# Where modulation's sums, the latents' products and head 0's evictions stand in a two-layer retention and attention kernel

## The chip, the cores and the metric

The kernel runs on one core of a Trainium2 chip, in one launch. The metric is the time of one execution on the device in microseconds (us). All arithmetic that the reference does is done on the chip in 32-bit numbers; a matmul of such numbers is made of three products of a high and a low part (high by high, high by low, low by high), so every operand is first split into `hi` and `lo`.

Five engines matter. PE does the matmuls and writes sums into PSUM banks. DVE and ACT do the elementwise work, read PSUM and make the high and low parts: ACT copies the high part, DVE subtracts it from the whole to get the low part. SP issues loads, POOL issues stores and some tiny powers. Each engine takes its instructions in the order of its own list, so an instruction that waits holds back all that stand behind it on that engine.

## The reference, cut to what matters

```python
c_act = silu(c)
for i in range(2):                       # layer 0: retention, layer 1: latent attention
    mod = c_act @ ada_w[i] + ada_b[i]    # modulation: 3 x 2048 numbers a layer
    shift, scale, gate = split(mod, 3)
    h = rmsnorm(x, norm_g[i]) * (1 + scale) + shift
    y = retention_branch(h) if i == 0 else mla_branch(h)
    x = x + gate * y
return rmsnorm(x, final_norm_g)
```

There are 512 tokens of width 2048. Retention has 8 heads: for each, queries and keys (2 x 256 columns) are turned by a rotary table; scores of keys and queries, times a decay, multiply the values (512 columns); the result is normalised over each head's columns and multiplied by a SiLU gate (512 columns), and all heads go through one output projection. Latent attention projects h to two latents of 512 columns, a rotary key and a gate of 2048 columns, expands the latents to 16 heads and does causal softmax attention.

`mod` is a matrix-vector product: each of its 128-row groups needs a load of 128 x 2048 weights, a product with `silu(c)` and a sum along the row. The kernel does it on DVE.

## The kernel before, in words

**Stages, in order of time.** First the tokens' norm, layer 0's first modulation, and head 0's `qk`, values and gates in one interleaved sweep over the width (to about 160 us). Then a list called `steps`, which is walked in order: head 5's `qk` as a plain step list (`qk_steps(5)`); for each head 1 to 4 fourteen narrow steps (`narrow_qk`) for its queries and keys, then sixteen steps for its values and gates (`heads_steps`); for heads 5, 6, 7 the sixteen alone; then plain steps for `qk` of heads 6 and 7; then four rounds of sixteen steps, n = 0 to 3, of the output projection (`round_steps`), beside which retention itself runs; then layer 1: gate columns in plain steps (`g2_steps`), the latents as sixteen steps again, two more groups of gates, attention, and the last projection.

**Sixteen steps: `seven_steps`** (L766 on). A product of 1024 by 1024 blocks is done with seven multiplications instead of eight. The first eight steps (u = 0 to 7, the first sweep) add to four pairs of banks: x and s, in the four banks tagged `acc`; z and y, in the four tagged `aux`. Two of each are used by every head, so a head's first product into a bank waits until the head before has emptied it. The second sweep, again u = 0 to 7, adds to x, y and s only; z has been copied out at its start. After u = 7 of the second sweep `finish` empties x and s by ACT (L641) and adds y to two saved tiles by DVE (L988, L990). In a first-sweep step the groups of three matmuls per bank are listed x, s, z, y (two banks each); for u = 0 the list is reordered to z, x, y, s, for the heads and for the latents (`"c"`, which come from the same function). The step's weights arrive as two tiles, e and o; `prepare` combines them on DVE and splits them (L802 to L809 first sweep, L814 to L819 second).

**Narrow steps** (`narrow_steps`, L852 on) do a head's queries and keys the same way with half-width products: per group of pairs one step for `b11`, then three steps (`o`, `a`, `b`) twice; two such groups make fourteen steps of 24 matmuls of 256 columns. The preparation of `a` needs four DVE combinations (L931 to L935) before its split (L874, L875).

**The walk over `steps`** (end of the function) writes, for step i and in this order: SP's weight loads for up to three units ahead and the loads set beside the step; the preparation (split) of the weights of steps up to i + `lead` (1, or 2 around the narrow steps) on DVE and ACT; the work set beside it under `form`; the step's matmuls, then matmuls set beside it (scores, values, transposes); then the DVE sums of modulation whose operands were fetched in the step before; then one load for each of the next step's `rows`; then the step's `follow` (evictions). Each block on an engine is queued behind the last instruction written for that engine. So `step.rows` is how many sums of modulation are done after that step, and their loads are written at the end of the step before.

**Modulation's sums.** `all_rows` yields 8 x 2 tiles for each of eight pieces: three pieces (48 sums) while heads 1 to 7 run, three (48 sums) in the rounds, two (32) with the last gates. One sum is L1074 (`mod<-mod,c_bm`, `c_odd` or `c_k4b`): it multiplies a tile of 128 x 1024 by `silu(c)` and sums the rows. Two buffers hold the tiles in the first two phases, so a load waits for the sum before last. In the second sweep of each of the heads 1 to 7 the steps u = 1 to 7 have `rows` = 1 (49 places for 48 sums). In rounds 0, 1, 2 all steps but 5 and 13 have it, and steps 0 to 5 of round 3, 48 in all.

**Retention beside the rounds.** `retention(h)` has fourteen pieces; even heads start at step 0 of a round, odd heads at step 4, heads 0 and 1 beside the `qk` of heads 6 and 7. Piece 6 are the scores (`s`), piece 8 decays them and splits them, piece 9 splits the values (`v`, L137 and L138) and multiplies (`y`), piece 10 is the normalisation: statistics of the four `y` banks on DVE (L1215, L1216), a power on POOL, and `yn` on ACT (L1227), which empties the banks; piece 12 transposes. So in a round the even head's scores follow the matmuls of step 6, its values those of step 9, and the odd head's scores those of step 10; they use the same four `aux` banks. A round's weights are `o_r`, split into `o_whi` (ACT) and `o_wlo` (DVE); steps 3, 7, 11 and 15 end with copies from banks to memory and back (L1323, L1320).

**Head 0's evictions.** Before the walk, four banks of head 0's `qk` and four of its gates are emptied by `keep_rows` (L639 to L642): ACT writes a tile, POOL stores it. For `qk` the tile is in turn one of six buffers `tmp` or one of two buffers `st` of a pool opened there, whose memory was the first stage's until then; `in_turn` chooses. The gates use `tmp`.

## Time and profile before

| what | value |
|---|---|
| time, median of 3 executions | 2176.03 us (2175.23 to 2176.48) |
| the profiled execution: time, and span from first to last instruction | 2175.93 us, 2174.2 us |
| PE busy | 2140.4 us, 98% |
| DVE busy | 1641.1 us, 75% |
| ACT busy | 1044.0 us, 48% |
| DMA | 440.34 MB, mean 203 GB/s |
| mean granted PE clock | 0.997 |

A row of a timeline reads: start in us from the span's start, duration in us, engine, line of the kernel, operation, tile written, tiles read, shapes, how many in a row, and in brackets how long the engine had been idle before it and what ended that. `SPq` is a load being issued. A matmul's end is modelled, and matmuls overlap: the next one starts before the recorded end of the one before.

### The profile page before, as it was taken

The numbers are of one execution on the slowest core, as the hardware profiler recorded it, in microseconds if no ns is written. First come the engines' busy times: TensorE is split into PE (matmuls) and PEld (weight loads), VectorE is DVE, ScalarE is ACT, GpSimd is POOL, SyncE is SP. The second block draws the span as 40 slices with busy tenths as digits, with TensorE's granted clock in tenths as the row PEclk, the third lists the DMA queues.
The fourth block names the chain that finished last, engine by engine and source line by source line (L and its number), as shares of the span: only waits on it lengthen the run. The fifth ranks groups of instructions, "written<-read, shape, count | busy, mean of one in ns | idle before, by whom it ended". The sixth has DMA issues, their size and how long they took to land. (4 is left out here: it accounts for less than half of the span.)

```text
span 2174.2 us, 29045 instructions
## 1 busy us (share of the span) xinstructions
PE 2140.4 (98%) x10782; PEld 1813.9 (83%) x10782; DVE 1641.1 (75%) x2411; ACT 1044.0 (48%) x1581; POOL 103.7 (5%) x175
## 2 busy tenths in 40 slices
PE   8999999999999999999999999999999999999997
PEld 6888989898987887888888787888788889888887
DVE  8988878888889889666777777767877677775545
ACT  6767344444444444434344444434444365664443
POOL 0000000010000000000000000010001000000000
PEclk9999999999999999999999999999999999999998
DMA  9965685767668778765656565753458623335333
GB/s 386 385 237 165 193 263 186 232 205 223 210 211 290 255 241 275 255 201 173 213 178 224 170 213 188 235 178 101 156 184 313 248 88 100 94 103 184 112 104 128
DMA packets 204848, 440.34 MB, mean 203 GB/s; under 512 B 19185, under 2 KB 56081, under 8 KB 200865
## 3 DMA queue, kind: packets, MB, share of 16 engines
q1 hardware_dynamic: 192640, 399.57, 55.8%
q0 software_dynamic: 11920, 38.91, 4.7%
q8 instruction: 84, 1.38, 0.3%
q14 instruction: 58, 0.48, 0.1%
q10 hardware_dynamic: 146, 0.01, 0.0%
HBM read 395.42 MB, written 43.00 MB: 202 GB/s over the span
## 5 line engine op out<-in xcount | busy, mean ns | idle before, releaser
L1372 PE MATMUL o<-o_h,o_whi 128*128 128x512 f32 (+1 forms) x496 | 192.2, 388 | 0.0
L1372 PE MATMUL o<-o_h,o_wlo 128*128 128x512 f32 (+1 forms) x496 | 191.4, 386 | 0.0
L1372 PE MATMUL o<-o_l,o_whi 128*128 128x512 f32 (+1 forms) x496 | 191.3, 386 | 0.0
L138 DVE TENSOR_TENSOR o_wlo<-o_r,o_whi 128x1024 fp32r<-128x1024 f32 x61 | 74.6, 1223 | 72.2 <-ACT o_whi L137 72.2
L1372 PEld LDWEIGHTS o<-o_h,o_wlo 128*128 128x128 f32 x496 | 93.2, 188 | 18.7
L1372 PEld LDWEIGHTS o<-o_h,o_whi 128*128 128x128 f32 x496 | 93.2, 188 | 18.3
L1372 PEld LDWEIGHTS o<-o_l,o_whi 128*128 128x128 f32 x496 | 93.2, 188 | 18.3
L163 PE MATMUL g<-h,g_h 128*128 128x512 f32 x232 | 90.7, 391 | 0.3 <-ACT g_h L137 0.3
L164 PE MATMUL g<-h,g_h 128*128 128x512 f32 x232 | 90.3, 389 | 0.0
L165 PE MATMUL g<-h,g_l 128*128 128x512 f32 x232 | 89.9, 390 | 0.1
L163 PE MATMUL qk<-hT,qk_h 128*128 128x512 f32 x192 | 75.0, 391 | 1.0 <-ACT qk_st L641 1.0
L164 PE MATMUL qk<-hT,qk_h 128*128 128x512 f32 x192 | 74.7, 389 | 0.0
L165 PE MATMUL qk<-hT,qk_l 128*128 128x512 f32 x192 | 74.6, 389 | 0.0
L137 ACT CAST o_whi<-o_r 128x1024 fp32r<-128x1024 f32 x61 | 63.6, 1053 | 20.1 <-issue 10.2
L353 DVE SCALAR_TENSOR_TENSOR aw<-aw,c_all 128x2048 f32<-128x2048 f32 x30 | 67.6, 2288 | 0.0
L138 DVE TENSOR_TENSOR o_w_lo<-o_w_raw,o_w_hi 128x1024 fp32r<-128x1024 f32 x32 | 39.0, 1221 | 37.1 <-ACT o_w_hi L137 37.1
L138 DVE TENSOR_TENSOR o_l<-o_in,o_h 128x1024 fp32r<-128x1024 f32 x24 | 29.3, 1223 | 48.2 <-ACT o_h L137 48.2
L1074 DVE SCALAR_TENSOR_TENSOR mod<-mod,c_bm 128x1024 f32<-128x1024 f32 x48 | 58.6, 1220 | 5.2 <-DMA mod<-in_ada_t_dram 5.2
L1074 DVE SCALAR_TENSOR_TENSOR mod<-mod,c_odd 128x1024 f32<-128x1024 f32 x48 | 58.5, 1219 | 0.0
L2238 PE MATMUL o<-o_l,o_w_hi 128*128 128x512 f32 (+1 forms) x160 | 55.5, 347 | 0.9 <-DVE o_l L138 0.9
L2238 PE MATMUL o<-o_h,o_w_hi 128*128 128x512 f32 (+1 forms) x160 | 55.7, 348 | 0.2 <-ACT o_h L137 0.2
L2238 PE MATMUL o<-o_h,o_w_lo 128*128 128x512 f32 (+1 forms) x160 | 55.4, 346 | 0.0
(1308 smaller groups left out, 6627.6 us busy)
## 6 DMA issues: line engine op xcount, KB each, us to landing
mod<-in_ada_t_dram SPq DMA_DIRECT2D x128, 512.0 KB, 5.6
o_r<-in_ret_w_out_dram SPq DMA_DIRECT2D x64, 512.0 KB, 4.6
aw<-in_ada_t_dram SPq DMA_DIRECT2D x30, 1024.0 KB, 7.9
g_r<-in_mla_w_in_dram SPq DMA_DIRECT2D x32, 512.0 KB, 4.6
o_w_raw<-in_mla_w_out_dram SPq DMA_DIRECT2D x32, 512.0 KB, 3.8
qk_r<-in_ret_w_in_dram SPq DMA_DIRECT2D x48, 256.0 KB, 3.2
qk_o_r<-in_ret_w_in_dram SPq DMA_DIRECT2D x32, 256.0 KB, 4.2
qk_r<-qk_d SPq DMA_DIRECT2D x32, 256.0 KB, 5.9
```

The costliest lines, as they stand in the source:

```text
L137: ACT.copy(hi, src)
L138: DVE.tensor_sub(lo, src, hi.bitcast(F32))
L163: PE.matmul(o, lhs[0], rhs[0], start=first and not seeded, stop=False, skip_group_check=seeded)
L164: PE.matmul(o, lhs[0], rhs[1], start=False, stop=False, skip_group_check=seeded)
L165: return PE.matmul(o, lhs[1], rhs[0], start=False, stop=last, skip_group_check=seeded)
L353: DVE.scalar_tensor_tensor(out=aw, in0=aw, scalar=1.0, in1=c_all, op0=ALU.mult, op1=ALU.mult, accum_out=col,)
L1074: DVE.scalar_tensor_tensor(out=aw, in0=aw, scalar=1.0, in1=silu_c[j], op0=ALU.mult, op1=ALU.mult, accum_out=mc[:, j, b : b + 1],)
L1372: PE.matmul(o, w[i][:, ki, c0 + b * P : c0 + (b + 1) * P], a[j], start=first and i + j == 0, stop=last and i == 1, skip_group_check=True,)
L2238: PE.matmul(banks2[b][:, cols], w[0][i][:, 0, b * P : (b + 1) * P], o2_moving(w, u, cols)[j], start=u + i + j == 0, stop=u == KD - 1 and i ...
```

## The change

There are four parts to it.

1. **The order of the first products.** In step u = 0 the order z, x, y, s stays for heads 1 to 4 only. Heads 5, 6 and 7 and the latents get the listed order x, s, z, y.
2. **Sums while the heads run.** The last step of each second sweep (u = 7) loses its sum, and the narrow steps 2 and 3 of heads 1 to 4 get one each: 7 x 6 + 4 x 2 = 50 places for the 48 sums.
3. **Sums in the rounds.** In rounds 0, 1 and 2 steps 1, 8 and 9 lose theirs (5 and 13 have none, as before), and steps 0, 3 and 7 get two. In round 3 the sum of step 1 is done after step 6 instead. The number stays 48.
4. **Head 0's evictions** of `qk` all go to `tmp`.

```diff
-    def seven_steps(h, block, form, raw_tile, part_tiles, finish, rows):
+    def seven_steps(h, block, form, raw_tile, part_tiles, finish, rows, free_first=False):
...
                     forms = [(x_, (0, 0), "b11"), (s_, 1, "t1"), (z_, (1, 1), "t4"), (y_, 2, "t2")]
-                    if u == 0:
+                    if u == 0 and free_first:
                         forms = [forms[i] for i in (2, 0, 3, 1)]
...
             lambda n, u, b: form(hT, sums1, n, u, b), *turns1, finish,
-            lambda second, u: int(second and u > 0),
+            lambda second, u: int(second and 0 < u < 7), h < 5,
...
             for step in block[:13]:
                 step.lead = 2
+            for i in (2, 3):
+                block[i].rows = 1
             block[10].ahead = 2
...
-    def light(block, which):
+    def light(block, which, n=1):
 
         for i in which:
-            block[i].rows = 1
+            block[i].rows = n
...
-        light(block, [i for i in range(16) if i not in (5, 13)])
+        light(block, (0, 2, 3, 4, 6, 7, 10, 11, 12, 14, 15))
+        light(block, (0, 3, 7), 2)
...
-    light(block, range(6))
+    light(block, (0, 2, 3, 4, 5, 6))
...
     for b in range(4):
-        queued(keep_rows, qk0[b], qk_d, b * P, f"qk0_st{b}", AF.Identity, in_turn(b))
+        queued(keep_rows, qk0[b], qk_d, b * P, f"qk0_st{b}", AF.Identity, tmp)
```

## The prediction

> **What bounds the kernel now.** The page comes first, for who is busy over the whole span:

> ```profile
> span 2174.2 us, 29045 instructions
> ...
> PE 2140.4 (98%) x10782; PEld 1813.9 (83%) x10782; DVE 1641.1 (75%) x2411; ACT 1044.0 (48%) x1581; POOL 103.7 (5%) x175
> ```

> PE is busy in all but 33.8 us. The matmuls are not changed in number or size, so the change can only fill or open pauses of PE. The view of waits, for PE alone, says whom PE waited for (total us, times, longest):

> ```profile
> PE s L163 <- ACT yn L1227: 3.4, 4, 1.1
> PE y L164 <- DVE v L138: 2.4, 3, 0.9
> ...
> PE sc L774 <- ACT sgs L1613: 1.2, 1, 1.2
> ...
> PE qk_m L870 <- DVE qk_a_l L875: 1.0, 2, 0.5
> ...
> PE qk_m L870 <- ACT qk_a_h L874: 0.7, 2, 0.3
> ...
> PE x L775 <- DVE vg_01e_l L806: 0.5, 3, 0.2
> ```

> These are the pauses the change can reach. The `s` and `y` rows lie in retention (scores and values of the heads), `sc` at the start of the latents' steps, `qk_m` in the narrow steps, `x` at the start of heads 5 to 7. All but `sc` end on DVE or on an ACT instruction fed by DVE, and DVE there also carries modulation's sums. The third view is the timeline around each of them.

> For the distance between matmuls I take the stretches view (PE busy and count, weight loads, DVE, ACT, POOL, granted clock, DMA share, GB/s):

> ```profile
> 1181.00:1189.00 8.00, 8.00 (x37) 6.61 (x36) 2.58 (x4) 5.69 (x9) 0.00 (x0) 1.00 0.72 247
> ...
> 2160.00:2174.00 14.00, 2.74 (x15) 2.07 (x13) 8.88 (x18) 1.85 (x4) 0.70 (x1) 0.61 0.74 281
> ```

> 37 matmuls in 8 us of an always busy PE are about 0.225 us from start to start. The trace's record of a matmul is longer than that, so a real stall is some 0.16 us more than the idle time printed. A step of 24 matmuls is 5.4 us. The second row is for later.

> **Part one: sums in retention.** Head 4 stands for heads 2, 4 and 6. Its scores follow step 6 of the round, its values step 9, and the scores of head 5 follow step 10. DVE, then ACT, SP and PE:

> ```profile
> 1179.73 1.22 DVE L1074 SCALAR_TENSOR_TENSOR mod<-mod,c_odd 128x1024 f32<-128x1024 f32 x1
> ...
> 1182.01 1.22 DVE L1074 SCALAR_TENSOR_TENSOR mod<-mod,c_odd 128x1024 f32<-128x1024 f32 x1
> ...
> 1188.66 1.22 DVE L138 TENSOR_TENSOR o_wlo<-o_r,o_whi 128x1024 fp32r<-128x1024 f32 x1 [5.42 <-ACT o_whi L137]
> ...
> 1196.31 1.22 DVE L1074 SCALAR_TENSOR_TENSOR mod<-mod,c_odd 128x1024 f32<-128x1024 f32 x1
> ...
> 1197.45 1.22 DVE L138 TENSOR_TENSOR o_wlo<-o_r,o_whi 128x1024 fp32r<-128x1024 f32 x1
> ...
> 1204.31 1.22 DVE L1074 SCALAR_TENSOR_TENSOR mod<-mod,c_odd 128x1024 f32<-128x1024 f32 x1
> ...
> 1205.45 1.22 DVE L138 TENSOR_TENSOR o_wlo<-o_r,o_whi 128x1024 fp32r<-128x1024 f32 x1
> ...
> 1210.95 0.16 DVE L1221 SCALAR_TENSOR_TENSOR nmr<-bn,gn_r 128x4 f32<-128x4 f32 x1 [1.12 <-POOL gn_r L133]
> ```
> ```profile
> 1195.57 1.05 ACT L137 CAST o_whi<-o_r 128x1024 fp32r<-128x1024 f32 x1
> 1196.52 2.17 ACT L137 CAST v<-v_r 128x512 fp32r<-128x512 f32 x4
> ...
> 1203.57 1.05 ACT L137 CAST o_whi<-o_r 128x1024 fp32r<-128x1024 f32 x1
> 1211.15 2.79 ACT L1227 ACTIVATE yn<-y,nmr,gn_r 128x512 f32<-128x512 f32 x4 [6.52 <-DVE nmr L1221]
> ```
> ```profile
> 1180.99 0.33 SPq L1069 DMA_DIRECT2D mod<-in_ada_t_dram  x1
> ```
> ```profile
> 1199.33 0.50 PE L164 MATMUL y<-v,sT 128*128 128x512 f32 x1 [0.92 <-DVE v L138]
> ...
> 1211.98 0.50 PE L163 MATMUL s<-qk_0p,qk_0p 128*128 128x512 f32 x1 [1.03 <-ACT yn L1227]
> ```
> ```profile
> DMA to landing us min/median/max: 3.6/5.6/10.0
> ```

> The four `mod` rows are the sums of steps 6, 7, 8 and 9. From 1188.66 to 1210.95 DVE works almost without a break, and the sums of steps 8 and 9 stand in that chain, 1.14 us each (1196.31 to 1197.45, 1204.31 to 1205.45). Before it DVE idles 5.42 us, since `o_whi` stands behind the copies that ACT makes at the end of step 7. The change takes the sums of steps 1, 8 and 9 out and pairs them with those of 0, 3 and 7; the pair of step 7 falls into that hole.

> Removing the first sum does not gain 1.14: `o_wlo` then waits for `o_whi`, which ends at 1196.62, so it starts at 1196.65 rather than 1197.45: 0.8, and `y` with it. The second sum is worth 1.14 less 0.34, for the next `o_wlo` meets its `o_whi`, which moves with the chain, ending near 1203.82: it starts at 1203.85 instead of 1205.45. From there `nmr` and `yn` follow 1.6 us earlier, and `s` starts at 1210.4 instead of 1211.98. PE itself would be there at about 1210.0 (now 1211.98 - 1.03 - 0.16, less the 0.8), so 0.4 us of stall stays and 1.6 go. Heads 2 and 6 have the same waits: the row of `y` counts 3, that of `s` counts 4, of which the short fourth lies before the rounds. Term: 3 x 1.6 = 4.8 us. The bounds are 0, if the moved sum pushes the chain by what it saves, and 6.5, all of these stalls (2.4 + 3.4 - 0.25 for the fourth + 6 x 0.16).

> What is moved is a load too. Two buffers hold the sums' operands, so step 7's second load waits for step 6's sum, to 1180.97, the moment at which the load of the row above was issued. It needs 3.6 to 10.0 us, median 5.6: landing near 1186.6, sum done by 1187.8, inside the hole that ends at 1188.66. SP stands meanwhile: the decay, two tiles of q and k, and the weights of three steps ahead are queued behind it, up to 10 us later than now. The decay and q and k are read after the `o_wlo` of 1188.66, the weights by the `o_whi` of 1195.57. For steps 0 and 3 the same holds: step 3 also ends with copies, and what step 0 delays on DVE is first needed two steps on. I put these at nothing; the covers are the hole and SP's lead. Round 3's sum, from step 1 to 6, meets no wait of PE at either place.

> **Part two: head 0's evictions.**

> ```profile
> 156.19 0.58 ACT L641 ACTIVATE qk_st<-qk 128x512 f32<-128x512 f32 x1
> 161.37 1.57 ACT L641 ACTIVATE qk_st<-qk 128x512 f32<-128x512 f32 x3 [4.61 <-DMA tables_d<-ret_cos]
> ```
> ```profile
> 162.02 0.50 PE L163 MATMUL qk<-hT,qk_h 128*128 128x512 f32 x1 [0.99 <-ACT qk_st L641]
> ```

> The second of four evictions waits 4.61 us until the store of the rotary table has left memory that its buffer takes over; PE stalls 0.99 + 0.16 for the bank. With the other buffers three are cleared by about 160.2, as PE finishes them: 1.15 us gone, bounds 0 (a buffer still in use) and 1.15. Eight evictions share six buffers, so the last two gates wait for stores; no matmul needs their banks soon, and ACT's next cast is for a step two steps off.

> **Part three: narrow steps and second sweeps.** In heads 1 to 4 the sum after the last second-sweep step goes, and two come into the narrow steps.

> ```profile
> 321.15 1.22 DVE L1074 SCALAR_TENSOR_TENSOR mod<-mod,c_bm 128x1024 f32<-128x1024 f32 x1
> ```
> ```profile
> 329.15 0.39 PE L870 MATMUL qk_m<-sums,qk_a_l 128*128 128x256 f32 x1 [0.52 <-DVE qk_a_l L875]
> ```

> Everything from 321.15 to the first `qk_a_l` is one DVE chain. It moves forward 1.05 (the next instruction still needs the last `y`). Twice, in narrow heads 2 and 4, PE waits there, 1.7 us by the two rows of waits plus 4 x 0.16: 2.3 to be had, 2 x 1.05 = 2.1 taken. The two sums that come in stand behind the preparations of narrow steps 4 and 5. DVE is then as late for step 5 as now, about half a microsecond before PE: bounds 0 and 2.3.

> Heads 5 to 7 start so (head 6; PE then DVE):

> ```profile
> 755.93 0.39 PE L774 MATMUL z<-vg_00o_h,hT 128*128 128x512 f32 x1
> ...
> 762.94 0.50 PE L775 MATMUL x<-vg_01e_l,hT 128*128 128x512 f32 x1 [0.18 <-DVE vg_01e_l L806]
> ```
> ```profile
> 756.07 1.22 DVE L1074 SCALAR_TENSOR_TENSOR mod<-mod,c_bm 128x1024 f32<-128x1024 f32 x1
> ...
> 761.66 1.22 DVE L806 TENSOR_TENSOR vg_01e_l<-vg_01e_r,vg_01e_h 128x1024 fp32r<-128x1024 f32 x1
> ```

> 27 matmuls lie between the two PE rows: 6.1 us of work in 7.0. Without the sum `vg_01e_l` ends near 761.85, and PE would reach it at 762.05. The order x, s, z, y also puts `y` last, away from the sums of m and y that it waits for. 0.8 each, 3 x 0.8 = 2.4; bounds 0 and 2.7.

> **Part four: the latents' order.**

> ```profile
> 1557.30 1.56 ACT L1613 ACTIVATE sgs<-g 128x512 f32<-128x512 f32 x3
> 1562.47 0.60 ACT L1613 ACTIVATE sgs<-g 128x512 f32<-128x512 f32 x1 [3.61 <-DMA sg_d<-sgs]
> ```
> ```profile
> 1563.12 0.50 PE L774 MATMUL sc<-vgc_00e_h,sums 128*128 128x512 f32 x1 [1.20 <-ACT sgs L1613]
> ...
> 1564.05 0.73 PE L774 MATMUL xc<-vgc_01e_h,h 128*128 128x512 f32 x2
> ...
> 1565.31 0.50 PE L775 MATMUL xc<-vgc_01e_l,h 128*128 128x512 f32 x1 [0.30 <-DVE vgc_01e_l L806]
> ```

> The fourth gate eviction has no buffer until a store lands, and clears the bank of the second `s` at 1563.07. Now that bank's three matmuls come last of 24. With x, s, z, y they come fourth of eight groups, and 12 matmuls (z, y) follow them: 2.7 us later, less the 0.30 + 0.16 stall of the next step and its slow start: 2.0. But the rows show that the built order is not the source's: the source has a bank's three products together, the trace has two `L774` ahead of a late `L775`. If the build moves z and y ahead of the late bank again, the cost is 0. I take 1.2, nearer the source's order.

> Sum: -4.8 - 1.15 - 2.1 - 2.4 + 1.2 = -9.25 us on the profiled execution, 2175.93, which is 0.1 under the median of 2176.03: 2166.7.

> **The rivals.**

> *The sums come back in retention.* If a double step's second load lands after 1187.4, its sum pushes the chain from 1188.66. After 8.2 us (landing at 1189.2, sum done at 1190.3) the 1.6 are lost and the result is 2166.7 + 4.8 = 2171.5; after the row's 10.0, 1.9 us more are lost in each round, 2177.2. Against it: the median, 5.6, is in time by 0.8. For it: SP sends six other loads right behind. Chance 0.12, half of it on either side of 2171.6.

> *SP's stand starves the values (slower).* Held to 1180.97, SP has 3.4 MB to bring before the last of v's four tiles is in: 13.8 us at the 247 GB/s of the stretch and some 2 us of latency, so near 1197; ACT casts the fourth tile at 1198.1 (1196.52 and three quarters of 2.17). At two thirds of the rate it lands 5.5 us behind that, in three rounds: 2175.93 - 4.45 (the other terms) + 16.5 = 2188. It decides from 1.5 us of lateness in a round, a rate under some 205 GB/s. For it: the margin is 1 us. Against: that stretch's DMA share is 0.72, so it had room. Chance 0.04.

> *The clock falls in the latents' pause.* In source order PE would pause some 3.2 us before the second `s`. The row 2160 to 2174 shows the granted clock at 0.61 where PE had little to do. If it stood there for as long as the pause, 3.2 x (1/0.61 - 1) = 2.0 us come on top of the 2.0: 2166.7 - 1.2 + 4.0 = 2169.5. Against: PE was idle for 11 of those 14 us. Chance 0.08. [...]

> *The build puts it back.* Order on each engine is chosen in the build, as shown above; if it undoes the moves, 2176. Against: the sums keep their steps in every row seen. Chance 0.06.

> **How the numbers follow.** The forecast, 2166.7, has 0.70. The range goes from all upper bounds with latents at nothing (-6.5 - 1.15 - 2.3 - 2.7 = -12.65: 2163.3) to the first rival's lower price, 2171.5. No change means within 0.2%, 4.35 us, about what a measurement of this kernel can tell. Faster: 0.70 + 0.06 + 0.08 = 0.84; same: 0.06 + 0.06 = 0.12; slower 0.04.

> **What would show it.** Right: no wait of `qk` on `qk_st`; none of `qk_m` on `qk_a`; `y` on `v` under 0.3 us and `s` on `yn` under 0.5 each in the rounds; sums in pairs inside the DVE hole before the end of steps 3 and 7; `sc` in a longer pause than 1.20. Wrong: DVE waiting for `mod` loads just ahead of `o_wlo` after a double step, ACT waiting for v's tiles, or a clock under 1.00 after the latents' pause.

## The result, and the profile after

| | before | after |
|---|---|---|
| time, median (range, executions) | 2175.91 us (2175.23 to 2176.48, 4) | 2163.82 us (2163.18 to 2164.31, 4) |
| profiled execution: time, span | 2175.93, 2174.2 us | 2164.31, 2162.5 us |

The ratio is 0.9944, with a 95% interval from 0.9927 to 0.9962: 12.1 us less by the medians, 11.6 us between the profiled executions. The forecast was 2166.7, in a range from 2163.3 to 2171.5, so the result lies in the range, 0.5 us above its lower end. Time and direction came out; one step of the working, the latents' order, did not, and it takes most of the experiments.

The page of the changed kernel, the span and the busy times:

```profile
span 2162.5 us, 29040 instructions
...
PE 2137.0 (99%) x10782; PEld 1814.0 (84%) x10782; DVE 1641.6 (76%) x2411; ACT 1044.6 (48%) x1581; POOL 103.7 (5%) x175
```

The work is the same, 10782 matmuls on PE and 2411 instructions on DVE. Only pauses went. The view of waits of the changed kernel, PE alone (total us, times, longest):

```profile
PE s L163 <- ACT yn L1229: 1.0, 4, 0.3
...
PE x L775 <- DVE vg_01e_l L806: 0.3, 1, 0.3
...
PE x L775 <- DVE vg_17o_l L816: 0.2, 1, 0.2
```

The wait of `s` on `yn` fell from 3.4 to 1.0; the rows of `y` on `v`, `qk` on `qk_st`, `qk_m` on `qk_a` and `sc` on `sgs` are gone. A sharper tool is to follow the same matmul through both timelines. Both kernels have the same 10782 matmuls in almost the same order, so the lead of the changed kernel can be read at any of them, and a step in the lead is the gain of one place (differences of the rounded stamps; 0.01 either way is rounding):

| matmul | start before | start after | lead | gained since the row above |
|---|---|---|---|---|
| `qk`, first stage | 128.23 | 128.55 | -0.32 | |
| `qk` behind head 0's evictions | 186.18 | 185.21 | 0.97 | 1.29, evictions |
| end of head 1 | 321.19 | 320.20 | 0.99 | |
| `qk_m`, narrow steps of head 2 | 352.68 | 350.57 | 2.11 | 1.12 |
| `x`, end of head 3 | 553.95 | 551.96 | 1.99 | |
| narrow steps of head 4 | 599.62 | 596.52 | 3.10 | 1.11 |
| `x`, end of head 4 | 672.79 | 669.71 | 3.08 | |
| `x`, end of head 7 | 908.35 | 904.13 | 4.22 | 1.14, starts of heads 5 to 7 |
| scores of head 2 (round 0) | 1063.05 | 1058.83 | 4.22 | |
| scores of head 4 (round 1) | 1176.98 | 1171.17 | 5.81 | 1.59 |
| scores of head 6 (round 2) | 1291.57 | 1284.17 | 7.40 | 1.59 |
| transposes of head 7 | 1342.76 | 1333.78 | 8.98 | 1.58 |
| `zc`, first product of the latents | 1556.99 | 1548.03 | 8.96 | |
| `yc`, sixth step of the latents | 1591.33 | 1580.52 | 10.81 | 1.85, latents |
| last gates | 1702.34 | 1690.98 | 11.36 | 0.55 |
| last projection | 2157.74 | 2146.38 | 11.36 | |

The rounds gained 4.76 us where 4.8 were forecast. The latents gained 1.85 where 1.2 were to be lost.

How the rounds did it shows on DVE in round 1 of the changed kernel (timeline), and on SP:

```profile
1179.97 1.23 DVE L1076 SCALAR_TENSOR_TENSOR mod<-mod,c_odd 128x1024 f32<-128x1024 f32 x1 [2.54 <-DMA mod<-in_ada_t_dram]
...
1182.84 1.22 DVE L138 TENSOR_TENSOR o_wlo<-o_r,o_whi 128x1024 fp32r<-128x1024 f32 x1 [1.64 <-ACT o_whi L137]
...
1190.84 1.23 DVE L138 TENSOR_TENSOR o_wlo<-o_r,o_whi 128x1024 fp32r<-128x1024 f32 x1 [0.26 <-ACT o_whi L137]
...
1198.04 1.23 DVE L138 TENSOR_TENSOR o_wlo<-o_r,o_whi 128x1024 fp32r<-128x1024 f32 x1 [0.26 <-ACT o_whi L137]
...
1203.55 0.16 DVE L1223 SCALAR_TENSOR_TENSOR nmr<-bn,gn_r 128x4 f32<-128x4 f32 x1 [1.12 <-POOL gn_r L133]
```
```profile
1175.18 0.33 SPq L1071 DMA_DIRECT2D mod<-in_ada_t_dram  x1
```

The second load of the pair was issued at 1175.18, and DVE waited 2.54 us for it, but inside the hole: the sum starts at 1179.97 and its result is read at 1181.12, and DVE then still idles 1.64 us for `o_whi`. The next two `o_wlo` now wait for ACT (0.26 each) and not for sums. Over the three rounds DVE waits 17.4 us for such loads, where it waited 0.0 before; PE's waits behind it shrank all the same. From the first `o_wlo` to `nmr` there are 20.7 us, where the kernel before took 22.3 (1188.66 to 1210.95).

And the latents, PE, ACT and POOL of the changed kernel:

```profile
1548.03 0.39 PE L774 MATMUL zc<-vgc_00o_h,h 128*128 128x512 f32 x1
...
1548.96 0.50 PE L774 MATMUL xc<-vgc_00e_h,h 128*128 128x512 f32 x1
...
1552.54 0.39 PE L774 MATMUL sc<-vgc_00e_h,sums 128*128 128x512 f32 x1
```
```profile
1551.66 0.60 ACT L1616 ACTIVATE sgs<-g 128x512 f32<-128x512 f32 x1 [1.78 <-DMA sg_d<-sgs]
```
```profile
1549.20 1.60 POOL L1618 DMA_DIRECT2D sg_d<-sgs  x3 [41.70 <-ACT sgs L1616]
```

The build moved products about: the order it made is z, x, x, s, z, y, s, y. So the second `s` starts 4.51 us after the first `z`, not the 6.13 of before (1556.99 to 1563.12). Yet nothing waits there, because the fourth gate eviction comes sooner: its store landed in time to start it at 1551.66, 2.46 us after the first store was issued (1549.20), where before it took 4.30 us (1558.17 to 1562.47). Why a store should land 1.8 us sooner is the question that the order of products does not answer by itself.

### The profile page after: what moved, and what is told of

It is laid out like the page before. It is cut to its first block, busy times and chain, and to the rows that moved or that the text cites. A ratio compares the mean times of both kernels' runs of the same rounds, so it can differ in the third digit from the quotient of the medians.

```text
span 2162.5 us, 29040 instructions
## 1 busy us (share of the span) xinstructions
PE 2137.0 (99%) x10782; PEld 1814.0 (84%) x10782; DVE 1641.6 (76%) x2411; ACT 1044.6 (48%) x1581; POOL 103.7 (5%) x175
## 4 chain that ended last, share of the span: by engine, by line
PE 85%; DVE 6%; issue 4%; ACT 2%; DMA 2%; POOL 1%; SPq 0%; DVEq 0%; POOLq 0%; ACTq 0%
PE o L1374 14%; PE qk_m L870 7%; PE o L2241 4%; PE x L775 2%; PE y L775 2%; PE y L776 2%; PE y L774 2%; PE x L776 2%; PE x L774 2%; PE s L775 2%; PE s L776 2%; PE s L774 2%; PE qk L412 2%; PE o L165 2%; PE o L164 2%
## 5 line engine op out<-in xcount | busy, mean ns | idle before, releaser
L138 DVE TENSOR_TENSOR o_wlo<-o_r,o_whi 128x1024 fp32r<-128x1024 f32 x61 | 74.6, 1223 | 49.5 <-ACT o_whi L137 49.4
L163 PE MATMUL g<-h,g_h 128*128 128x512 f32 x232 | 90.6, 390 | 0.3 <-ACT g_h L137 0.3
L164 PE MATMUL g<-h,g_h 128*128 128x512 f32 x232 | 90.3, 389 | 0.0
L163 PE MATMUL qk<-hT,qk_h 128*128 128x512 f32 x192 | 74.9, 390 | 0.0
L164 PE MATMUL qk<-hT,qk_h 128*128 128x512 f32 x192 | 74.7, 389 | 0.0
L137 ACT CAST o_whi<-o_r 128x1024 fp32r<-128x1024 f32 x61 | 63.5, 1051 | 20.2 <-issue 10.2
L1076 DVE SCALAR_TENSOR_TENSOR mod<-mod,c_odd 128x1024 f32<-128x1024 f32 x48 | 58.5, 1220 | 17.4 <-DMA mod<-in_ada_t_dram 17.4
L138 DVE TENSOR_TENSOR o_w_lo<-o_w_raw,o_w_hi 128x1024 fp32r<-128x1024 f32 x32 | 39.0, 1220 | 36.9 <-ACT o_w_hi L137 36.9
L138 DVE TENSOR_TENSOR o_l<-o_in,o_h 128x1024 fp32r<-128x1024 f32 x24 | 29.3, 1223 | 48.2 <-ACT o_h L137 48.2
```

What stands on the lines that cost most here:

```text
L138: DVE.tensor_sub(lo, src, hi.bitcast(F32))
L163: PE.matmul(o, lhs[0], rhs[0], start=first and not seeded, stop=False, skip_group_check=seeded)
L164: PE.matmul(o, lhs[0], rhs[1], start=False, stop=False, skip_group_check=seeded)
L1076: DVE.scalar_tensor_tensor(out=aw, in0=aw, scalar=1.0, in1=silu_c[j], op0=ALU.mult, op1=ALU.mult, accum_out=mc[:, j, b : b + 1],)
```

## The experiments

Times are medians with range and number of executions; the ratio is to the kernel before, measured beside it. That kernel itself read 2175.91 in the first measurement and 2176.18, 2176.98 and 2176.52 in the later ones, so a difference of up to 1 us between medians of different measurements shows nothing by itself; the leads locate smaller ones. A lead in the text is worked out like that of the table, against the profiled execution of before.

### One part at a time

**Sums of the rounds alone**, on the kernel before:

```diff
-        light(block, [i for i in range(16) if i not in (5, 13)])
+        light(block, (0, 2, 3, 4, 6, 7, 10, 11, 12, 14, 15))
+        light(block, (0, 3, 7), 2)
...
-    light(block, range(6))
+    light(block, (0, 2, 3, 4, 5, 6))
```

> Only the sums of retention's rounds are moved; the rest is the kernel before. By the forecast's term (3 x 1.6 us) the time falls by 4.8 us; the pauses of PE counted in the trace of the changed kernel say 4.6. In the profile the waits of y on v and of s on yn in the three rounds shrink to under 0.3 us each. By the rival (the sums come back through a late second load) the gain is under 2 us and DVE waits for loads of mod just ahead of o_wlo.

Measured: 2170.58 us (2169.01 to 2171.65, 6), ratio 0.9972 (0.996 to 0.9983), 5.6 us less. The steps of the lead at rounds 0, 1, 2 are 1.59, 1.57 and 1.59: 4.75 us. Waits of PE in this kernel:

```profile
PE s L163 <- ACT yn L1227: 1.0, 4, 0.3
...
PE y L164 <- DVE v L138: 0.3, 2, 0.2
```

The term of the forecast holds by itself, and the sums do not come back.

**Second sweeps and narrow steps alone**, all orders as before:

```diff
-            lambda second, u: int(second and u > 0),
+            lambda second, u: int(second and 0 < u < 7),
...
+            for i in (2, 3):
+                block[i].rows = 1
```

> Only the sum after the last second-sweep step is taken out of heads 1 to 7, and two are put into the narrow steps of heads 1 to 4; all orders stay as before. By the forecast's terms the narrow steps give 2.1 us and the starts of heads 5 to 7 2.4 us: -4.5. By the reading of the trace of the changed kernel the starts of heads 5 to 7 gain far less, since the sum of the step before then waits for its load and holds up the last weights, so -2.1 and about 0.3 us for each of three heads: -3.0. Pauses on qk_a are gone by both.

Measured: 2172.66 us (2169.97 to 2173.11, 11), ratio 0.9982 (0.9973 to 0.9991), 3.5 us less, between the two expectations and nearer to -3.0. Lead: 1.13 and 1.12 at the two narrow heads, 1.19 over heads 5 to 7. Waits of PE:

```profile
PE sc L774 <- ACT sgs L1615: 1.6, 1, 1.6
...
PE x L775 <- DVE vg_17o_l L816: 0.6, 2, 0.4
PE z L775 <- DVE vg_00o_l L809: 0.3, 1, 0.3
```

The narrow steps give what was forecast. At the heads' starts one wait takes the place of another. The wait of 1.6 us on `sgs` is in the latents, which this change does not touch.

**Head 0's evictions alone:**

```diff
-        queued(keep_rows, qk0[b], qk_d, b * P, f"qk0_st{b}", AF.Identity, in_turn(b))
+        queued(keep_rows, qk0[b], qk_d, b * P, f"qk0_st{b}", AF.Identity, tmp)
```

> Only head 0's evictions are given other buffers. By the forecast's term 1.15 us less: 2174.8 beside 2175.9, and the pause of 0.99 us ahead of the first matmul of qk is gone, with no new one. By the rival that the gates' evictions then wait for stores and hold up ACT's casts, 0 to +1.

Measured: 2174.81 us (2172.64 to 2177.64, 11), ratio 0.9993 (0.9985 to 1.0002), 1.4 us less, too little for the interval to tell from nothing. The trace tells: the wait of `qk` is gone and the lead steps by 1.28 us at that place. The same execution lost 1.50 us of lead in the latents, so that its span, 2174.2, is that of before; this led to what follows.

### The latents: the order, or the store?

**The old order put back in the changed kernel**, in the latents alone:

```diff
-        latent_rows, lambda second, u: 0,
+        latent_rows, lambda second, u: 0, True,
```

> The changed kernel, with z, x, y, s put back in the first step of the latents alone. By the forecast's term (the new order costs 1.2 us) it is 1.2 us faster than the changed kernel, 2162.6. By the theory that the new order itself brought the latents' gain, the pause of 1.2 us before the second s returns, and with it the next step's 0.3: 1.4 to 1.8 us slower, 2165.4. By the theory that a store which landed 1.8 us sooner brought the gain (2.4 us after its issue instead of 4.2), the order makes no difference so long as the first store lands in about 2.4 us: within 0.4 us of the changed kernel, and a pause on sgs only where the first store takes 4 us.

Measured: 2166.68 us (2165.7 to 2167.28, 5), ratio 0.9954 (0.9941 to 0.9966), 2.9 us above the changed kernel. ACT, PE and the stretches of this kernel (stretches: PE busy and count, weight loads, DVE, ACT, POOL, granted clock, DMA share, GB/s):

```profile
1553.62 0.60 ACT L1616 ACTIVATE sgs<-g 128x512 f32<-128x512 f32 x1 [4.15 <-DMA sg_d<-sgs]
```
```profile
1554.27 0.50 PE L774 MATMUL sc<-vgc_00e_h,sums 128*128 128x512 f32 x1 [1.74 <-ACT sgs L1616]
```
```profile
1555.00:1556.00 1.00, 1.00 (x5) 0.49 (x3) 0.81 (x1) 1.00 (x2) 0.05 (x1) 0.89 0.42 160
1556.00:1557.00 1.00, 0.93 (x2) 0.50 (x2) 1.00 (x2) 0.10 (x1) 0.00 (x0) 0.50 0.27 102
1557.00:1558.00 1.00, 1.00 (x4) 0.76 (x3) 1.00 (x2) 0.00 (x0) 0.00 (x0) 0.50 0.00 0
1558.00:1559.00 1.00, 1.00 (x4) 0.81 (x3) 0.93 (x3) 0.77 (x1) 0.00 (x0) 0.50 0.54 57
1559.00:1560.00 1.00, 1.00 (x5) 0.77 (x5) 1.00 (x2) 0.59 (x2) 0.00 (x0) 0.91 0.74 291
```

Two things are seen. The pause came back with the order (1.74 us), since the store took 4.7 us again: the order or something tied to it does set the landing. And the pause has a tail: from 1555.8 to 1559.2 PE's clock was granted at 0.50, by estimate some 1.7 us more (half of these 3.4 us). The same tail is in the profiles of the second and third kernels above (in the second the four stretches from 1561 to 1565 read 0.72, 0.50, 0.50 and 0.57).

What is tied to the order? DMA traffic of this kernel in a stretch of 1.6 us that begins just before the stores, and of the changed kernel in a stretch of 2.1 us at the same place (queue, kind: packets, MB, share of 16 engines):

```profile
q0 software_dynamic: 38, 0.16, 25.6%
q8 instruction: 1, 0.02, 7.1%
q1 hardware_dynamic: 17, 0.02, 3.5%
```
```profile
q0 software_dynamic: 74, 0.26, 34.3%
q1 hardware_dynamic: 23, 0.04, 4.6%
```

In the old order one packet of 16 KB, kind `instruction`, comes while the first store is under way (it starts at 1550.21 and takes 1.83 us on one of the 16 engines); in the new order it starts at 1551.20, when the first store's packets are through. The page of the changed kernel has 84 such packets beside 10782 matmuls, one for every 128 on the mean. That they bring PE's own list of instructions in pieces is the author's estimate from this count; no view says it. The DMA records of the old-order trace show the store's packets around it. A store of 256 KB is made of 64 packets of 4 KB and 16 closing marks of 4 bytes, by their number one for each engine. By 1550.75, 60 of the first store's 64 packets have started and 15 of its marks are written. The last four packets start only from 1552.02 on, as the 16 KB packet ends (1552.04); the sixteenth mark comes at 1553.03 and the store lands at 1553.52. The trace of before shows the same: 15 marks by 1560.13, the 16 KB packet from 1559.81 to 1561.18, the sixteenth mark at 1561.87. In the changed kernel all 16 marks are written by 1551.16, before the 16 KB packet starts at 1551.20; it ends at 1552.42, and there the second and third store, whose sixteenth marks come at 1553.42 and 1554.05, take 4.16 and 4.25 us, for which nothing waits. Whether the packet and not the order decides can be tested by moving the packets and leaving the order alone.

**The old order with the packets moved** by small matmuls without use at the start:

```diff
+    for _ in range(20):
+        PE.matmul(c_ps[3][:, 0:P], ones, ones, start=True, stop=True)
     for j, ps in enumerate(c_ps):
...
-        latent_rows, lambda second, u: 0,
+        latent_rows, lambda second, u: 0, True,
```

> The changed kernel with z, x, y, s put back in the latents (the run before of that kind: 2166.7, first store 4.7 us to landing) and 20 small matmuls without use at the very start, where PE waits for its first input. They move PE's stream of instructions on by 20 matmuls, so that the packet of 16 KB that brings its next instructions comes before the first gate store and not 1.4 us after its issue. By the theory that this packet holds up the store, the store lands in about 2.4 us, the pause of 1.74 us before the second s and the half clock behind it are gone, and the time is 2 to 3 us below that run: 2164. By the theory that the order itself sets the landing, or that it is luck, nothing changes: 2166.7.

Measured: 2166.29 us (2164.68 to 2167.16, 5), ratio 0.9951 (0.9937 to 0.9965): by the total no change. But the total has a new term, the start (below). In the trace the packet comes 9.5 us ahead of the stores (the profile records each small matmul twice, 40 more in all), and ACT and PE read:

```profile
1552.77 0.60 ACT L1618 ACTIVATE sgs<-g 128x512 f32<-128x512 f32 x1 [1.79 <-DMA sg_d<-sgs]
```
```profile
1553.89 0.39 PE L776 MATMUL sc<-vgc_00e_h,sums 128*128 128x512 f32 x1
```

The first store lands in 2.36 us with the old order, the second `s` does not wait, and the clock stays at 1.00. The lead steps by 1.83 us in the latents, against 1.85 with the new order.

**The new order with the same 20 matmuls**, the control:

> The changed kernel with the same 20 matmuls at the start and the new order in the latents: what the 20 matmuls do by themselves. The packet then comes ahead of the stores, all of which land in 2.3 to 3 us: within 0.5 us of the changed kernel, 2163.3 to 2164.3, by every theory; another time is what the start costs or gains.

Measured: 2166.53 us (2164.9 to 2167.62, 5), ratio 0.9953 (0.9941 to 0.9966). The expectation was wrong: the 20 matmuls cost some 2.7 us by the medians (1.2 us of lead before 128 us in the profiled execution). Where the other 1.5 us of the medians went is not located. Since the two kernels differ in the order alone, the order makes no difference here once the packet is out of the way: 2166.29 beside 2166.53, a step in the lead of 1.83 beside 1.80. What the start lost shows on PE and ACT, first in the changed kernel, then in this one:

```profile
5.09 7.16 PE L437 MATMUL c_ps<-c_all,ones 1*128 1x512 f32 x8 [5.09 <-DMA c_all<-in_c_dram]
7.16 0.60 ACT L470 ACTIVATE c_all<-c_ps 128x512 f32<-128x512 f32 x1 [1.03 <-PE c_ps L437]
```
```profile
1.06 6.26 PE L467 MATMUL c_ps<-ones 128*128 128x128 f32 x40 [1.06 <-DVE mhalf L125]
7.25 3.69 PE L437 MATMUL c_ps<-c_all,ones 1*128 1x512 f32 x8
8.41 0.60 ACT L472 ACTIVATE c_all<-c_ps 128x512 f32<-128x512 f32 x1 [2.80 <-PE c_ps L437]
```

The small matmuls hold PE until 7.25; in the changed kernel its input let it start at 5.09. ACT stands at its first `c_all` until 8.41 instead of 7.16, the squares of x behind it in ACT's list come later, and the first sums of squares on PE (`x_sums`) start at 16.08 instead of 15.19.

**The new order with 4 such matmuls** (the same edit, `range(4)`, order as changed), which put the packet back on the store:

> The changed kernel with 4 such matmuls at the start: the packet comes some 0.9 us earlier, about 1.1 us after the first store's issue, where all runs of the old order had it. By the theory of the packet the first store lands in 4 us or more in the new order too, the fourth eviction is late by 2 us, the second s waits some 1.5 us, and the time is 1.5 to 3.5 us above the changed kernel. By the theory that the order sets the landing: 2.4 us, within 0.3 us of the changed kernel.

Measured: 2166.6 us (2166.11 to 2168.2, 5), ratio 0.9956 (0.9943 to 0.9968), 2.8 us above the changed kernel, as expected by the theory of the packet. POOL, ACT and PE:

```profile
1549.02 1.61 POOL L1620 DMA_DIRECT2D sg_d<-sgs  x3 [41.75 <-ACT sgs L1618]
```
```profile
1553.26 0.60 ACT L1618 ACTIVATE sgs<-g 128x512 f32<-128x512 f32 x1 [3.55 <-DMA sg_d<-sgs]
```
```profile
1553.90 0.50 PE L776 MATMUL sc<-vgc_00e_h,sums 128*128 128x512 f32 x1 [1.39 <-ACT sgs L1618]
```

All traces with the gates' buffers as in the kernel before, side by side (packet's start after the issue of the first store; time from issue to landing of that store; step of the lead in the latents):

| kernel | order | packet | landing | step of the lead |
|---|---|---|---|---|
| before | z, x, y, s | +1.64 | 4.19 | 0 |
| rounds alone | z, x, y, s | +1.27 | 3.74 | 0.46 |
| second sweeps and narrow steps alone | z, x, y, s | +1.26 | 4.63 | -1.60 |
| evictions alone | z, x, y, s | +1.20 | 4.54 | -1.50 |
| old order back | z, x, y, s | +1.42 | 4.73 | -1.78 |
| old order, 20 matmuls on | z, x, y, s | -9.51 | 2.36 | 1.83 |
| after | x, s, z, y | +2.00 | 2.36 | 1.84 |
| heads' order back (below) | x, s, z, y | +2.06 | 2.36 | 1.85 |
| pair in step 8 (below) | x, s, z, y | +2.05 | 2.37 | 1.86 |
| new order, 20 matmuls on | x, s, z, y | -9.28 | 2.36 | 1.80 |
| new order, 4 matmuls on | x, s, z, y | +1.15 | 4.13 | 0.08 |

The landing goes with the packet and not with the order, 11 times of 11.

**A buffer more, so that no eviction waits for a store.** First on the kernel before:

```diff
-            sgs = l2_tile("sg", 3, f"sgs_{gi}_{b}")
+            sgs = l2_tile("sg", 3, f"sgs_{gi}_{b}") if b < 3 else tmp(f"sgs_{gi}_{b}")
```

> The kernel before with the same buffer for the fourth gate eviction, and z, x, y, s as it was. If all that the latents gained is the wait of the second s on a store and what comes of it (1.2 to 1.7 us of pause, 0.3 in the next step, and in some executions 3.4 us at half clock, 1.7 us), this gives the same as the new order gave: 1.5 to 3.4 us less than the kernel before, and no stretch at half clock. If the order brings something of its own, less than 1 us.

Measured: 2172.68 us (2171.78 to 2174.28, 11), ratio 0.9983 (0.9974 to 0.9992), 4.3 us less, more than was expected; the step in the latents is 2.35 us though the first store took 4.08 us, and the clock stays. So the wait for the store and what comes of it is all that the latents had to give. Another 0.57 us of lead is gained at the gates ahead of the latents, where PE no longer waits for `g_h`; all three kernels with this buffer have that step and no other has. What is left of the 4.3 us is not located by this one pair of profiles.

Then on the changed kernel, the same edit:

> The changed kernel; the fourth gate eviction of each four goes to a buffer of its own, so that it waits for no store. If a store landing early was luck in the profile of the changed kernel, its usual run pays for the late ones, and this one is 0.5 to 1.5 us faster. If the new order already covers the wait, within 0.3 us of the changed kernel; the wait of sgs on sg_d is gone by both.

Measured: 2162.67 us (2162.59 to 2163.34, 5), ratio 0.9938 (0.9925 to 0.9951): 1.15 us below the changed kernel by the medians, with overlapping intervals. The wait of the fourth eviction is gone and no longer hangs on where a packet falls. The gain over the changed kernel is not one of the latents: their step is 1.95 us, there 1.84; 0.57 us come at the gates ahead of them, as above, and 0.6 over heads 5 to 7, a place that varies by itself (below). This has the lowest median of all the kernels. Beside the old order with the same buffer (above) it also shows what the order costs where no eviction waits: the step is 2.35 us with z, x, y, s and 1.95 with x, s, z, y, in which PE's fourth matmul (1547.70) waits for the first gate eviction, some 0.37 us. The old order with the buffer in the changed kernel was not run.

### The starts of heads 5 to 7

**The old order put back in heads 5 to 7:**

```diff
-            lambda second, u: int(second and 0 < u < 7), h < 5,
+            lambda second, u: int(second and 0 < u < 7), True,
```

> The changed kernel with z, x, y, s put back in the first step of heads 5 to 7 alone; latents keep the new order. By the forecast's side remark (the new order keeps y away from the sums that it waits for) it is slower than the changed kernel, by 0.2 to 0.6 us. By the reading of the traces (in the old order the build put 27 matmuls ahead of the first one that needs vg_01e_l, in the new one 25; each is 0.2265 us) the three waits of x on vg_01e_l go, 0.3 us each and more at head 5: 0.6 to 1.0 us faster, 2163.0; the waits of x on vg_17o_l stay by both.

Measured: 2163.97 us (2163.69 to 2164.78, 5), ratio 0.9943 (0.9929 to 0.9957): the changed kernel's time. Waits of PE:

```profile
PE x L775 <- DVE vg_17o_l L816: 0.8, 2, 0.6
PE z L775 <- DVE vg_00o_l L809: 0.3, 1, 0.3
```

The waits on `vg_01e_l` went out of the view, but not for the reason expected: here too the build puts 25 matmuls ahead of the first that needs it, and at head 6 that one comes 5.96 us after the head's first, in the changed kernel 5.99. The 27 stand in the four kernels whose second sweep keeps its last sum (before, rounds alone, evictions alone, the buffer on the kernel before), the 25 in all others, in either order. A wait on `vg_00o_l` came at head 5, and those on `vg_17o_l` were longer here. Both theories missed; the order in these heads makes no difference that this measurement tells.

**One sum fewer at the end of heads 6 and 7**, with the buffer of above:

```diff
-            lambda second, u: int(second and 0 < u < 7), h < 5,
+            lambda second, u: int(second and 0 < u < (6 if h > 5 else 7)), h < 5,
```

> The changed kernel with the buffer for the fourth gate eviction (2162.7 in its run) and heads 6 and 7 without the sum after the last but one step of the second sweep, whose load landed late there and held up vg_17o_l. By the reading of the trace the waits of x on vg_17o_l go at the starts of head 7 and after it, 0.2 to 0.5 us: 2162.3. By the rival that these waits come from vg_17o's own cast and weights, no change: 2162.7.

Measured: 2163.18 us (2161.96 to 2163.38, 5), ratio 0.9938 (0.9926 to 0.9951). Waits of PE:

```profile
PE x L775 <- DVE vg_17o_l L816: 0.5, 1, 0.5
PE x L775 <- DVE vg_01e_l L806: 0.4, 1, 0.4
```

The one wait on `vg_17o_l` in this view is at the end of head 4 (670.11 us), which kept its sum. The end of head 6, which lost it, is free of the wait, but the view of the kernel with the buffer alone, where head 6 kept it, has no wait on `vg_17o_l` either. It is no gain that can be measured, and one profile is too little to put the wait down to the load.

### The hole in DVE

**The pair in step 8 instead of step 7**, on the changed kernel:

```diff
-        light(block, (0, 3, 7), 2)
+        light(block, (0, 3, 8), 2)
```

> The changed kernel with the pair of sums in the rounds at step 8 instead of step 7, which has one: the same count, one sum fewer in DVE's hole and two in the chain that leads to y and s. By the theory that the hole carries the gain of the rounds, y and s come later by 0.9 + 1.14 us in each round: 6 us more than the changed kernel, 2169.9. If what counted was only that sums left the steps before the scores' own, not where they went, it is within 1 us of the changed kernel. DVE waits for no load of mod here, since the step before has freed the operand.

Measured: 2171.59 us (2169.28 to 2172.86, 10), ratio 0.9975 (0.9965 to 0.9984), 7.8 us above the changed kernel by the medians, 6.7 by the two differences to the kernel before. PE and DVE in round 1, and its stretches:

```profile
1195.76 0.50 PE L164 MATMUL y<-v,sT 128*128 128x512 f32 x1 [2.10 <-DVE v L138]
```
```profile
1183.94 1.23 DVE L138 TENSOR_TENSOR o_wlo<-o_r,o_whi 128x1024 fp32r<-128x1024 f32 x1 [5.42 <-ACT o_whi L137]
...
1191.60 1.22 DVE L1076 SCALAR_TENSOR_TENSOR mod<-mod,c_odd 128x1024 f32<-128x1024 f32 x1
1192.74 0.08 DVE L1076 DVE_READ_ACCUMULATOR mod<-mod,c_odd 128x1 f32 x1
1192.74 1.22 DVE L1076 SCALAR_TENSOR_TENSOR mod<-mod,c_odd 128x1024 f32<-128x1024 f32 x1
1193.88 0.08 DVE L1076 DVE_READ_ACCUMULATOR mod<-mod,c_odd 128x1 f32 x1
1193.88 1.22 DVE L138 TENSOR_TENSOR o_wlo<-o_r,o_whi 128x1024 fp32r<-128x1024 f32 x1
```
```profile
1197.00:1198.00 1.00, 1.00 (x3) 0.77 (x3) 1.00 (x2) 0.00 (x0) 0.00 (x0) 0.50 0.74 264
```

From `o_wlo` to `o_wlo` there are 9.94 us, in the changed kernel 8.00 (1182.84 to 1190.84): 1.94, forecast 0.9 + 1.14. By the lead, rounds 0, 1 and 2 lose 1.96, 3.06 and 3.00 us against the changed kernel: the first is the chain alone (a pause of 1.63 us, the clock stays), in the others a pause of 2.10 us is followed by a clock of 0.50 for 3.4 us, and about 1 us more is lost. So the place of the pair carries the gain, and 6 us was too little by what comes with that slow stretch.

## Why the prediction was right, and where it was wrong

**What bounds.** Right. PE's matmuls stayed and its pauses shrank, at the places that the view of waits had named.

**Part one, sums in retention.** Right in mechanism and size: -4.8 forecast, -4.76 in the pair of traces, -4.75 alone. The two covers named for the moved load held: its sum ended at 1181.1, 1.7 us before the hole did (0.9 was forecast), and no instruction of ACT waited for v's tiles. The one rival, that the sums come back, would have needed a landing 1.7 us later. One sign that had been named for it did appear, DVE waiting for a load of `mod` after a double step (2.54 us); it meant nothing, since `o_wlo` behind it still had to wait for ACT. The rival that ends slower, values starved by SP, did not appear, and no run tests it; the pair in step 8 makes the values late by another route, DVE. The 2 us of latency in its working was an estimate. The trace of before bears it out: a load of 512 KB that ran alone there (`o_r`, issued at 1237.15) took 3.60 us to landing, of which its bytes make 1.3 at the 399 GB/s of its fastest slices, so 2.3 are left.

**Part two, evictions.** Right: -1.15 forecast, 1.29 in the lead, 1.28 alone.

**Part three, narrow steps.** Right: -2.1 forecast, 1.12 + 1.11 in the lead. The two sums that came in cost nothing there.

**Part three, starts of heads 5 to 7.** The term was too large: -2.4 forecast as 3 x 0.8, 1.14 in the pair of traces. The mechanism is the named one, the chain on DVE became shorter by 1.02 us (to the end of `vg_01e_l` from the head's first matmul: 5.93 us, before 6.95). DVE and PE at head 6 of the changed kernel:

```profile
757.10 1.22 DVE L806 TENSOR_TENSOR vg_01e_l<-vg_01e_r,vg_01e_h 128x1024 fp32r<-128x1024 f32 x1
```
```profile
758.38 0.50 PE L775 MATMUL x<-vg_01e_l,hT 128*128 128x512 f32 x1
```

But the step "27 matmuls lie between" did not carry over: without the last sum the build puts only 25 ahead of the first that needs `vg_01e_l`, in either order, which takes 0.45 back, and the sum after the last but one step waits for its load longer than before (1.28 us, before 0.77), so that `vg_17o_l` is late at the end of heads 5 and 6. In the profiles that have the shorter sweep the lead grows by 0.62 to 2.92 us over these heads (median 1.4 of ten), in three that do not by 0.24 to 0.84: the place varies by itself, and about 1 us is the change's. The side remark on the order is not borne out: with the old order put back these heads cost the same.

**Part four, the latents' order.** This step failed: "12 matmuls (z, y) follow them: 2.7 us later ... I take 1.2". The second `s` did come earlier in PE's list, as argued (4.51 us after the first z, before 6.13), and the build did move z and y only partly. But the argument held the fourth eviction fixed at its place of before, 5.48 us after the first `zc`, and it came after 3.63 us, because the first store landed in 2.36 us instead of 4.19. The experiments show why: a 16 KB packet no longer fell on that store. With the packet in the old place the new order gains 0.08 us, near the bound "0" that was given for a build that moves z and y ahead; with the packet elsewhere both orders gain 1.8. So the gain of 1.85 is real and repeats in each new-order trace that leaves the packets alone, but it is not the order's own: for the forecast it was luck, since nothing in its working looked at the packets. A cost of the order is there too, but it is another than the one forecast: 0.4 us, PE's wait at the fourth matmul, seen where no eviction waits. That the order moves the packet by 0.4 to 0.8 us may come from the same wait for the first gate eviction, which the new order meets after 3 matmuls (1548.96) and the old one not at all; it explains 0.37 us at most, and this is argued, not tested.

**The clock's rival.** It did not come in this kernel: no such pause is left in the latents, so the sign "`sc` in a longer pause than 1.20" did not come either, and the clock is on record at 1.00 from 23.15 to 2153.06. In three kernels with the old order a clock of 0.50 did follow the pause, after 1.55 to 1.74 us of it and not the 3.2 that the rival assumed. By the prediction's own rows the pause in source order would have been 1.20 + 0.16 + 2.7 = 4.1 us; 3.2 is 1.20 plus the net cost of 2.0, from which the next step's stall is taken off, and that is no part of the pause.

**The last gates.** 0.55 us of the lead was in no term. All later traces have it, those of single parts of the change too, so it most likely belongs to the one profiled execution of before (its first store at 1680.66 took 6.34 us, in the changed kernel 5.69) and not to the change.

Sum: 1.29 + 1.12 + 1.11 + 1.14 + 4.76 + 1.85 + 0.55 makes 11.82, less 0.32 at the start and 0.14 of small changes between: 11.36 of lead. Of the 2.4 us by which the forecast fell short, the latents make +3.05, the gates +0.55, and the heads -1.26. So the sum came out as near as it did in part because two misses, +3.05 and -1.26, offset each other.

## What to carry to other kernels

Work that has to stand on a busy engine goes into the hole where that engine waits for someone else, and its load should land before the hole ends (no run here had a late one): here the same pair of sums was free in one step and cost 7 to 8 us one step on. Follow the same instruction through two timelines before explaining a gain: the steps of the lead say which place gave it, and a gain at a place whose change ought to cost means that something else moved. Where an eviction waits for a store, try a buffer more before a better order of what comes behind: the buffer gave 2.35 us in the latents, the order by itself 0.08, and the landing of the same store lay anywhere from 2.36 to 4.73 us without a line of the transfer being changed.

## What the runs showed of the hardware that was not expected

**Five pauses of 1.55 to 2.10 us were followed by half the clock.** Idle times of 1.55, 1.65, 1.74 and 2.10 us (twice) ahead of a matmul were each followed by 3.4 us at 0.50, which began 1.1 to 1.5 us after PE went on. Those of 1.20 and 1.39 were not, nor was one of 1.63. So the length of the pause alone does not part them, and what else decides was not shown.

**At the start the same matmuls took nearly twice as long in the changed kernel as later.** Its records of the clock begin only at 23.15 us, and the stretches before that read 1.00; the matmuls say otherwise. Twelve `warm` matmuls from 19.11 take 2.91 us, and eight of them from 23.35, at 1.00 on record, 1.06. Its eight `c_ps` take 7.16 us, and 3.69 in the new-order kernel with 20 small matmuls ahead, whose stretches read 1.00 from 5 to 11 us, 0.51 from 11 to 25 and 1.00 from 25 to 30. So the changed kernel's clock stood near half at its start, by estimate from these times, and with the small matmuls ahead the full clock came early and went again. Why it fell near 11 was not followed up.
